# The second layer's gate by GpSimd and ScalarE, and a count that starts at zero with each list of products

## The chip, the cores and the metric

The kernel runs on one core of one Trainium2 chip. The metric is the device time of the program in microseconds (us). The core has five engines with a queue each: TensorE (PE) multiplies matrices, VectorE (DVE) and ScalarE (ACT) work on tiles element by element, GpSimd (POOL) does too, and SyncE (SP) issues the transfers between the memory of the chip and SBUF.

## What is computed

A decoder trunk of two layers on 256 rows of 2048 features, in fp32. Each layer takes three vectors of 2048 numbers from a condition `c`, by one product with a weight of 2048 x 6144:

```
mod = silu(c) @ ada_w[layer] + ada_b[layer]
shift, scale, gate = split(mod, 3)
h = x * (1 + scale) + shift
x = layer_norm(alpha * x + (1 + gate) * mixer(h))
```

The first layer's mixer is a state-space scan (Mamba-2) between two large projections. After it the stream gives one shared set of keys and values (`wk`, `wkv`), and the second layer's mixer is attention over them in three dilations, with a gate path. `gate` of the second layer is needed only in the last step of the kernel.

## The kernel before

Every weight is read in pieces of 128 x 1024 fp32 (512 KB, tile `raw`, six buffers). `split` makes two fp32r tiles of a piece: ScalarE rounds it to `whi` (L126), VectorE subtracts to get the rest `wlo` (L127); each has four buffers. TensorE then multiplies high by high, low by high and high by low. `tm_chunk` (L228 to L230) takes 512 output columns: a piece of it is 12 matmuls of 512 columns. `cm_wide` (L176, L178) takes 256 columns with tiles the other way round.

The products for `mod` are not made on TensorE. A column block of 128 outputs is a tile `araw` (128 x 2048, 1 MB); VectorE multiplies it with `cb_`, which holds silu(c) on every partition, and adds up along the row, in one instruction (`ada_dot`, L310; a second short one reads the accumulator). `ada_load` (L289) fetches the tile; its pools give `araw` two buffers.

`queue(pool, cols)` puts a list of such products into `jobs`, and loads the first at once; each job loads the next column and multiplies its own. `background(n, every)` is called once for each weight piece: it adds `n` to the count `state[0]`, and while that is `every` or more and there are jobs, it takes `every` off and runs one job. There are three lists:

- In the scan's stage, from g = 1 on: the first 8 blocks of the first layer's gate, then a blank and `gate_out(0, 0, 8)`. Rate (1, 8). `drain` at g = 6 runs what is left.
- In the output projection `wout` (chunks n = 0 to 3 of 512 columns, 16 pieces each, the last four of n = 3 held apart without a call), after chunk 0: the other 8 gate blocks, two blanks and `gate_out(0, 8)`, then the first 8 blocks of the second layer's scale and shift. Rate (1, 2).
- In the keys and values: the other 24 blocks of scale and shift, the 16 blocks of the second layer's gate (the second gate), a blank and `gate_out(1)`. Rate (8, 15), over 12 blocks of 4 pieces (`cm_join`) and 4 chunks of 8 (`values[2:]`), 80 calls in all.

`gate_out` adds the bias (L328), transposes the gate on TensorE into a row (L334), copies it (L337) and stores it to the chip's memory (L338); it is read back, spread over the partitions, as `gt` (L86), by which the residual (L851) multiplies a chunk's result. The transpose is pinned behind the weight matmul that was written last before it (`recent[0]`).

The order in which the program is written is not the order in which it runs. `arrange` puts all instructions of the program into an order of its own: a planner with a price for each instruction builds due times from the end, schedules forward, and then tries some 250 seeded random changes of the priorities and keeps what its model likes best. What the written order fixes is the rotation of the buffers and the pins. The planner's price of an operation on GpSimd is

```
return 0.2 + n / 400, 0.2 + n / 370, None, 0
```

in us, for n elements of a row; for ScalarE it is 0.19 + n / 1175 and for VectorE 0.152 + n / 960. When the tiles of the keys and values stage are given back, the pool of the attention stage (`pc2`) takes their place and waits for all their users. `cb_` is overwritten with the attention's bias (L1020) when its last reader is done. At the end of the keys and values stage VectorE and ScalarE also make the second layer's `h` (L1003, L1004, L253, L254).

Of the kernel before, what the change touches and what calls it, by code (L numbers as in the profile page):

```python
# [14 lines left out]
AF = mybir.ActivationFunctionType  # L15
ALU = mybir.AluOpType
# [55 lines left out]
def trunk(ctx, tc, xT, x, ada0, crow, par, cst, bias, lnrow, ada, wdt, win, wsub, wout, wkv, wk, wbin, wbout, out):  # L72
    nc = tc.nc
    del PINS[:]
    V, S, T = nc.vector, nc.scalar, nc.tensor
# [13 lines left out]
    cb_ = cons.tile([P, D], F32, name="cb_")  # L89
# [22 lines left out]
    def note(what, m):  # L112
        noted.setdefault(what, []).append(m.ins.name)
# [35 lines left out]
    state, recent = [0], [None]  # L149
# [136 lines left out]
    def ada_load(pool, layer, kind, ct):  # L286
        raw = pool.tile([P, D], F32, name="araw", bufs=2)
        for c_ in ada_loads(layer, kind, ct):
            m = nc.sync.dma_start(raw[:, c_], ada[layer, KIND.index(kind), ct][:, c_])  # L289
            note((kind, ct, layer), m)  # L290
        return raw

    def ada_parts(layer, kind, ct):

        if layer or kind == "gate" or ct > 1:
            return [slice(0, D)]
        return [slice(768 * i, 768 * i + 768) for i in range(2)] if ct else [slice(0, 512), slice(512, 1024), slice(1024, 1280)]

    def ada_loads(layer, kind, ct):

        return [slice(0, 1024)] if layer == ct == 0 and kind != "gate" else ada_parts(layer, kind, ct)

    def ada_dot(layer, kind, ct, raw, first=None, rest=None):

        j = KIND.index(kind)
        to = mod[layer][:, ct, j:j + 1]
        cuts = ada_parts(layer, kind, ct)
        n = len(cuts)
        if n == 1:
            V.scalar_tensor_tensor(raw, raw, 1.0, cb_, op0=ALU.mult, op1=ALU.mult, accum_out=to)  # L310
            return
        sums = ada_sums(ct, n)
        for i, c_ in enumerate(cuts):
            part = rest[:, j] if ct == 0 and i == 2 else raw[:, c_]
            note(("dot", ct), V.scalar_tensor_tensor(part, part, 1.0, cb_[:, c_], op0=ALU.mult,
                                                     op1=ALU.mult, accum_out=sums[:, j, i:i + 1]))
        if kind == "shift":
            V.tensor_copy(sums[:, :, n], adab[:, 0, ct, 0:2])
            m = mod[0][:, ct, 0:2]
            note(("dot", ct), V.tensor_reduce(m, sums, axis=AX.X, op=ALU.add))  # L320
            note(("dot", ct), V.tensor_tensor(m, first[1 - ct][0][:, :, 0], m, op=ALU.add))

    def ada_sums(ct, n):
        return mod[ct][:, :2 * n + 2, 2].rearrange("p (j i) -> p j i", j=2)
# [14 lines left out]

    def queue(pool, cols):  # L340

        loaded = [ada_load(pool, *cols[0])]

        def step(i):
            raw = loaded.pop(0)
            if i + 1 < len(cols):
                loaded.append(ada_load(pool, *cols[i + 1]))
            ada_dot(*cols[i], raw)

        jobs.extend(lambda i=i: step(i) for i in range(len(cols)))  # L350
# [12 lines left out]
    with ExitStack() as cA:  # L363
# [33 lines left out]
        with ExitStack() as cS:  # L397
# [99 lines left out]
            with ExitStack() as c0:  # L497
# [3 lines left out]
                cols = [(0, kind, kt) for kt in range(KT) for kind in ("scale", "shift")]  # L501
# [12 lines left out]
                def h_step():  # L514

                    _, kind, kt = cols[h_step.i]
                    raw = raws[h_step.i]
                    h_step.i += 1
                    if kind == "scale" and kt % 2 == 0 and kt:
                        fetch_x(kt)  # L520
                    ada_dot(0, kind, kt, raw, first, rest)
                    fetch()
                    while late:
                        late.pop()()
                    if kind == "shift":
                        if kt > 1:
                            ada_bias(0, slice(kt, kt + 1), slice(0, 2))
                        t = pe.tile([P, L], F32, name="htmp")
                        if kt > 1:
                            S.activation(t, xts[kt // 2][:, kt % 2, :], AF.Identity, bias=shift(0, kt), scale=scale(0, kt))  # L530
                            S.activation(hhi[:, kt, :], t, AF.Copy)
                        else:
                            note("hhi", S.activation(hhi[:, kt, :], xts[0][:, kt, :], AF.Identity, bias=shift(0, kt), scale=scale(0, kt)))
                            note(("dot", kt), V.tensor_scalar(t, xts[0][:, kt, :], scale(0, kt), shift(0, kt), op0=ALU.mult, op1=ALU.add))
                        late.append(lambda: note("hlo", V.tensor_tensor(hlo[:, kt, :], t, hhi[:, kt, :].bitcast(F32),
                                                                        op=ALU.subtract)))
# [272 lines left out]
            for g in range(G - 1):  # L809
                if g == 1:  # L810
                    queue(wp1, [(0, "gate", kt) for kt in range(KT // 2)])
                    jobs.extend([lambda: None] + [lambda: gate_out(0, 0, KT // 2)])
                if g == 6:
                    drain()
                if g % 2 == 1:
                    product("bc", g + 1)
                product(*(("xs", g + 1) if g < G - 2 else ("z", G - 2)))
                if rs is not None:
                    stage3(g - 1, rs)
                st1 = stage1(g)  # L820
                if g < G - 2:
                    product(*(("z", g + 1) if g < G - 3 else ("xs", G - 1)))
                rs = stage2(g, *st1)
# [63 lines left out]
        for n in range(4):  # L887
            ps = tm_chunk(wout[n], lambda kt: yhi[kt // 16][:, kt % 16, :], lambda kt: ylo[kt // 4][:, kt % 4, :],
                          nk=2 * KT, rate=(1, 2) if n else (0, 1), pre=None if n else y_ahead,
                          keep=[[pa.tile([P, 1024], F32R, name=f"y{2 * i + j}") for j in range(2)] for i in range(HELD)] if n == 3 else ())  # L890
            if n == 0:
                queue(pn, [(0, "gate", kt) for kt in range(KT // 2, KT)])
                jobs.extend([lambda: None] * 2 + [lambda: gate_out(0, KT // 2)])
                queue(pn, cols1[:8])
            gt = pn.tile([P, 512], F32, name="gt")
            bcast(gt, gated[0], 512 * n)
            c = slice(512 * n, 512 * n + 512)
            for b in range(2):
                xr = pn.tile([P, 512], F32, name="xr", bufs=2)
                nc.sync.dma_start(xr, x[b * P:b * P + P, c])  # L900
                residual(c, ps[b], b, (gt, u[b][:, c]), xr, [st[b][:, n, :]])
            if n == 2:
                root_ahead(2, 1)
# [917 lines left out]
```

## Time and profile before

| | |
|---|---|
| median of 3 runs | 1234.2 us (1233.13 to 1235.16) |
| the profiled execution, its own time | 1232.24 us |
| its span, first to last instruction | 1230.5 us |
| busy PE / DVE / ACT / POOL | 1217.1 / 1056.3 / 698.5 / 0.2 us |
| granted TensorE clock | 1.0 |
| moved by DMA | 358.30 MB, mean 291 GB/s |
| products of `ada_dot` in one instruction (L310) | 92, 2285 ns each |

The span is what the profile shows between the first and the last instruction; some 2 us of the device time lie around it. Line numbers are those of the kernel before. "Idle before" a group is the time that its engine stood before those instructions, with the one that ended the wait behind an arrow.

### The profile page before, as it was taken

To read this page: it belongs to the slowest core of one execution; us is meant where nothing else is said; L and a number is where in the kernel's file an instruction comes from. 1 tells how busy PE (TensorE), PEld (TensorE's weight loads), DVE (VectorE), ACT (ScalarE), POOL (GpSimd) and SP (SyncE) were. 2 spreads that over 40 slices of the span, in tenths; PEclk is the share of its full clock that TensorE was granted. 3 is DMA by queue.
4 is the path that set the end of the run, shared out by engine and by line. 5 is a ranking of instruction groups with operands and counts; after the bars stand their busy time and mean duration, and the time that the engine had idled before them with its cause. 6 is when DMAs were issued, how large, how long until landed. Compare 5 with 4: busy or idle time off the path is not lost.

```text
span 1230.5 us, 17555 instructions
## 1 busy us (share of the span) xinstructions
PE 1217.1 (99%) x6449; PEld 1040.5 (85%) x6449; DVE 1056.3 (86%) x1454; ACT 698.5 (57%) x1041; POOL 0.2 (0%) x4
## 2 busy tenths in 40 slices
PE   8999999999999999999999999999999999999998
PEld 8889888888888888887888788888888889989876
DVE  6998997999999999999857699989986747858677
ACT  4655475687758587963335464435346645545551
POOL 0000000000000000000000000000000000000000
PEclk9999999999999999999999999999999999999999
DMA  9999986978799787789967699999996563462571
GB/s 369 422 420 423 421 326 218 334 252 299 277 354 354 250 277 277 240 330 379 378 209 264 219 378 402 367 385 372 386 376 230 188 190 120 151 193 85 191 272 68
DMA packets 90377, 358.30 MB, mean 291 GB/s; under 512 B 9674, under 2 KB 10410, under 8 KB 77236
## 3 DMA queue, kind: packets, MB, share of 16 engines
q1 hardware_dynamic: 90292, 357.20, 78.9%
q8 instruction: 50, 0.82, 0.3%
q14 instruction: 35, 0.29, 0.1%
HBM read 351.30 MB, written 5.86 MB: 290 GB/s over the span
## 4 chain that ended last, share of the span: by engine, by line
PE 76%; DMA 12%; DVE 8%; ACT 2%; issue 1%; SPq 0%; DVEq 0%; ACTq 0%
PE acc L176 18%; PE acc L229 14%; PE acc L230 14%; PE acc L228 14%; PE acc L178 9%; DMA raw<-in_win 7%; DVE wlo L127 3%; DMA araw<-in_ada 2%; PE py L794 2%; DVE araw L310 2%; DMA xt<-in_xT 2%; DMA raw<-in_wout 1%; DVE ylo L395 1%; PE aux L1056 1%; PE po L1084 1%
## 5 line engine op out<-in xcount | busy, mean ns | idle before, releaser
L126 ACT ACTIVATE whi<-raw 128x1024 fp32r<-128x1024 f32 (+1 forms) x393 | 410.0, 1049 | 348.3 <-PE acc L230 152.9
L127 DVE TENSOR_TENSOR wlo<-raw,whi 128x1024 fp32r<-128x1024 f32 (+1 forms) x393 | 473.1, 1211 | 109.2 <-ACT whi L126 102.8
L229 PE MATMUL acc<-wlo,act 128*128 128x512 f32 x860 | 328.4, 394 | 1.6 <-DVE wlo L127 1.6
L228 PE MATMUL acc<-whi,act 128*128 128x512 f32 x860 | 319.9, 394 | 0.1
L176 PE MATMUL acc<-act,whi 128*128 128x512 f32 x1024 | 267.2, 395 | 0.0
L230 PE MATMUL acc<-whi,act 128*128 128x512 f32 x620 | 233.8, 392 | 0.0
L310 DVE SCALAR_TENSOR_TENSOR araw<-araw,cb__72 128x2048 f32<-128x2048 f32 x92 | 210.2, 2285 | 5.1 <-DMA araw<-in_ada 4.8
L176 PEld LDWEIGHTS acc<-act,whi 128*128 128x128 f32 x1024 | 184.7, 189 | 31.6
L229 PEld LDWEIGHTS acc<-wlo,act 128*128 128x128 f32 x860 | 161.0, 188 | 36.0 <-DVE wlo L127 3.7
L228 PEld LDWEIGHTS acc<-whi,act 128*128 128x128 f32 x860 | 161.1, 188 | 33.1 <-issue 0.5
L178 PE MATMUL acc<-act,wlo 128*128 128x256 f32 x1024 | 150.9, 284 | 0.0
L178 PEld LDWEIGHTS acc<-act,wlo 128*128 128x128 f32 x1024 | 142.0, 190 | 8.6
L230 PEld LDWEIGHTS acc<-whi,act 128*128 128x128 f32 x620 | 116.5, 188 | 24.1 <-issue 0.4
L230 PE MATMUL acc<-whi,ylo 128*128 128x512 f32 x208 | 78.5, 391 | 0.0
L165 PE MATMUL acc<-act,wlo 128*128 128x256 f32 x192 | 49.0, 285 | 0.0
L164 PE MATMUL acc<-act,whi 128*128 128x256 f32 x192 | 47.4, 286 | 1.3 <-ACT whi L126 0.8
L230 PEld LDWEIGHTS acc<-whi,ylo 128*128 128x128 f32 x208 | 39.1, 188 | 7.9
L751 ACT ACTIVATE seg<-seg,cumT 128x128 f32<-128x128 f32 x128 | 39.8, 389 | 1.7 <-DMA seg<-cumd 1.7
L162 PE MATMUL acc<-act,whi 128*128 128x256 f32 x192 | 37.7, 285 | 0.0
L164 PEld LDWEIGHTS acc<-act,whi 128*128 128x128 f32 x192 | 35.1, 191 | 3.1 <-ACT whi L126 1.4
L165 PEld LDWEIGHTS acc<-act,wlo 128*128 128x128 f32 x192 | 35.8, 191 | 1.0 <-DVE wlo L127 0.2
L794 PEld LDWEIGHTS py<-xd,seg 128*128 128x128 f32 x256 | 31.8, 192 | 3.3 <-issue 0.7
(309 smaller groups left out, 1252.4 us busy)
## 6 DMA issues: line engine op xcount, KB each, us to landing
araw<-in_ada SPq DMA_DIRECT2D x92, 1024.0 KB, 7.5
raw<-in_win SPq DMA_DIRECT2D x140, 512.0 KB, 7.4
raw<-in_wout SPq DMA_DIRECT2D x64, 512.0 KB, 4.9
raw<-in_wbin SPq DMA_DIRECT2D x64, 512.0 KB, 3.6
raw<-in_wkv SPq DMA_DIRECT2D x48, 512.0 KB, 5.7
raw<-in_wk SPq DMA_DIRECT2D x48, 512.0 KB, 6.7
moved<-back SPq DMA_DIRECT2D x21, 512.0 KB, 6.4
crow<-in_crow SPq DMA_DIRECT2D x7, 1280.0 KB, 9.4
```

The lines of the kernel that those rows point to most:

```text
L126: a = S.activation(hi[:, c_], raw[:, c_], AF.Copy)
L127: m = V.tensor_tensor(lo[:, c_], raw[:, c_], hi[:, c_].bitcast(F32), op=ALU.subtract)
L164: note("product", T.matmul(o, hi[:, k, c_], ahi[:, kt, :], start=kt == k0 and n % 2 == 0, stop=False, skip_group_check=True))
L165: T.matmul(o, lo[:, k, c_], ahi[:, kt, :], start=False, stop=False, skip_group_check=True)
L176: recent[0] = T.matmul(ps[n], hi[:, k, c_], both[:, kt], start=first, stop=False, skip_group_check=True)
L178: T.matmul(ps[n][:, 0, :], lo[:, k, c_], high[:, kt, :], start=first, stop=False, skip_group_check=True)
L228: begin = T.matmul(ps[b], h_, hi[:, k, :], start=kt == k0, stop=False)
L229: T.matmul(ps[b], h_, lo[:, k, :], start=False, stop=False)
L230: end = T.matmul(ps[b], l_, hi[:, k, :], start=False, stop=kt == k1 - 1)
L310: V.scalar_tensor_tensor(raw, raw, 1.0, cb_, op0=ALU.mult, op1=ALU.mult, accum_out=to)
L751: m = S.activation(seg[:, hh, b, :], seg[:, hh, b, :], AF.Relu, bias=cumT[:, b, h0 + hh:h0 + hh + 1], scale=-1.0)
L794: T.matmul(py[:, e_], segs[hh // 4][:, hh % 4, b, :], xd[:, b, e_], start=True, stop=True)
```

## The change

In `ada_dot`, a gate block of the second layer is multiplied by GpSimd, in place, and then summed by a copy on ScalarE that adds up along the row. The 16 instructions of L310 with their accumulator reads become 16 multiplies on GpSimd and 16 copies with accumulator reads on ScalarE. In `queue`, the count is set to zero with each list, so that what was counted while there were no jobs is forgotten. (The second stage's two lists are queued one right behind the other; both set it.)

```diff
         cuts = ada_parts(layer, kind, ct)
         n = len(cuts)
+        if layer and kind == "gate":
+            nc.gpsimd.tensor_tensor(raw, raw, cb_, op=ALU.mult)
+            S.activation(raw, raw, AF.Copy, accum_out=to)
+            return
         if n == 1:
             V.scalar_tensor_tensor(raw, raw, 1.0, cb_, op0=ALU.mult, op1=ALU.mult, accum_out=to)
             return
...
     def queue(pool, cols):
 
-        loaded = [ada_load(pool, *cols[0])]
+        loaded, state[0] = [ada_load(pool, *cols[0])], 0
```

## The prediction, made before the changed kernel ran

> **What bounds the kernel now.** I read the page's table of engines first, then the busy time by stretches, then the chain of waits where a stretch shows lost TensorE time, and last the groups inside the stretch in which the moved work runs.
>
> ```profile
> PE 1217.1 (99%) x6449; PEld 1040.5 (85%) x6449; DVE 1056.3 (86%) x1454; ACT 698.5 (57%) x1041; POOL 0.2 (0%) x4
> ```
>
> TensorE is busy 99% of the span, but ends of matmuls are modelled, so the count per stretch is the better sign. In the stretches the columns are PE, its weight load, DVE, ACT, POOL (instructions behind x), granted clock, DMA share, GB/s.
>
> ```profile
> 160.00:350.00 190.00, 189.91 (x953) 159.91 (x953) 179.58 (x266) 133.64 (x213) 0.00 (x0) 1.00 0.81 288
> 350.00:550.00 200.00, 199.53 (x1001) 167.09 (x1000) 197.25 (x305) 147.06 (x244) 0.00 (x0) 1.00 0.81 290
> 550.00:600.00 50.00, 48.08 (x212) 39.24 (x211) 44.90 (x49) 19.97 (x21) 0.00 (x0) 1.00 0.96 371
> 600.00:650.00 50.00, 50.00 (x222) 41.43 (x222) 33.28 (x32) 19.68 (x19) 0.00 (x0) 1.00 0.74 266
> 838.00:880.00 42.00, 42.00 (x237) 36.83 (x236) 39.05 (x41) 19.66 (x26) 0.00 (x0) 1.00 1.00 376
> 880.00:921.00 41.00, 41.00 (x182) 33.98 (x182) 35.23 (x32) 18.00 (x19) 0.00 (x0) 1.00 0.99 391
> 921.00:942.00 21.00, 21.00 (x95) 17.40 (x94) 10.59 (x12) 9.12 (x10) 0.00 (x0) 1.00 0.72 239
> 942.00:966.00 24.00, 24.00 (x116) 20.10 (x115) 21.70 (x40) 21.81 (x42) 0.00 (x0) 1.00 0.59 195
> ```
>
> From 600 to 650 us, 222 matmuls, nearly all 512 columns wide, fill 50 us: 0.225 us each is the full pace. From 880 to 921 us there are 182, again 0.225 us each. So where the second gate's products run, TensorE loses nothing, although VectorE is 86 to 93% busy there. The one stretch behind the opening that loses time is 550 to 600 us: 212 matmuls, and 1.92 us idle. Two waits make it up, and the chain of waits runs through them:
>
> ```profile
> 560.98 0.73 PE L229 MATMUL acc<-wlo,act 128*128 128x512 f32 x2 [0.70 <-DVE wlo L127]
> 570.65 0.27 PE L334 MATMUL aux<-cc,mod 128*8 128x128 f32 x1 [1.21 <-DVE mod L328]
> ```
> ```profile
> 563.23 5.96 DMA raw<-in_wout
> ...
> 570.34 0.18 DVE mod L328
> ...
> 570.65 0.27 PE aux L334
> ```
> ```profile
> 566.99 2.29 DVE L310 SCALAR_TENSOR_TENSOR araw<-araw,cb__72 128x2048 f32<-128x2048 f32 x1 [1.58 <-DMA araw<-in_ada]
> ```
>
> L334 is the transpose in `gate_out` for the second half of the first layer's gate. It stands in TensorE's in-order queue before its input is there: the last dot product starts at 566.99, late by its own load, and TensorE stands 1.21 us.
>
> **The reset of the count.** `background` adds to the count also when `jobs` is empty. Counting the calls in the code: 17 before the first list, 104 when the first stage is over, of which its 10 jobs use 80; 24 are left. The second list has a job per 2, so its first call pops (24+1)/2 = 12 jobs: all eight gate products, two blanks, `gate_out` and one more. That pins the transpose only behind the first piece of chunk n=1, and the planner puts it as early as 570.65. From zero, `gate_out`, the 11th job, comes at call 22, the 6th piece of chunk n=2.
>
> ```profile
> 576.46 0.29 SPq L338 DMA_DIRECT2D gated<-row  x1
> ...
> 609.54 0.33 SPq L86 DMA_DIRECT2D gt<-gated  x1
> ```
> ```profile
> 649.63 0.68 DVE L851 TENSOR_TENSOR u<-acc,gt 128x512 f32<-128x512 f32 x1
> ```
> ```profile
> DMA to landing us min/median/max: 5.9/6.3/6.6
> ```
>
> Chunk n=2 ends near 649.6, its first residual. A piece is 12 matmuls, 2.7 us; with ten pieces left after the 6th the transpose cannot stand before about 649.6 - 27 = 623. Behind it come a copy, the store of the row and the load of gt, for which two landings of up to 6.6 us are a generous price: 623 + 14 = 637, 12 us before the residual. On SP's queue the gt load moves from 609.54 to about 630, behind the row's store; weight loads behind it are held for at most one landing, 6.6 us, against six buffers of raw (16 us of TensorE). I cost that at nothing. Gain: the 1.21 us wait goes. What is late next is the 0.70 us wait on wlo, which hangs on a weight load among the same gate loads; it may go as well (bounds of the term: 0 to -1.92; I take -1.2, the wait that the pin removes).
>
> The first list starts at zero instead of 17: its two first products no longer come at once, and its 9th and 10th job fall to `drain` at g=6. The dots are 8 x 2.3 us of VectorE either way, in stretches where TensorE loses 0.09 and 0.47 us; bounds -0.5 to +0.5, taken as 0. The third list starts at zero instead of 24 + 44 - 38 = 30, at 8 per call and 15 per job: its last job, `gate_out(1)`, moves from call 75 of 80 to call 79, that is from the third to the seventh piece of the last chunk, four pieces or 11 us.
>
> ```profile
> L334 PE MATMUL aux<-cc,mod x3: 270/271/272, 427.3 to 949.6; 128*8 128x128 f32 x2, 128*16 128x128 f32 x1
> ```
>
> 949.6 becomes about 960. Its result is read only at the very end, so that costs nothing as long as the sums are there by then.
>
> **The moved products.** Sixteen products leave VectorE. From 840 to 925 us, and from 942 to 966:
>
> ```profile
> L127 DVE TENSOR_TENSOR wlo<-raw,whi 128x1024 fp32r<-128x1024 f32 x31 | 37.9, 1223 | 8.8 <-ACT whi L126 8.1 <-PE acc L178 0.5
> L310 DVE SCALAR_TENSOR_TENSOR araw<-araw,cb__72 128x2048 f32<-128x2048 f32 x16 | 36.6, 2285 | 0.4 <-DMA araw<-in_ada 0.4
> L126 ACT ACTIVATE whi<-raw 128x1024 fp32r<-128x1024 f32 x31 | 32.9, 1062 | 38.3 <-PE acc L230 24.1 <-PE acc L176 11.4 <-DVE wlo L127 1.9
> ...
> L958 ACT ACTIVATE vt<-acc 128x512 f32<-128x512 f32 x4 | 2.4, 592 | 2.2 <-PE acc L230 2.2
> ```
> ```profile
> L254 DVE TENSOR_TENSOR act<-htmp,act 128x256 fp32r<-128x256 f32 x16 | 6.3, 420 | 0.0
> ...
> L1004 DVE SCALAR_TENSOR_TENSOR htmp<-act,mod,htmp 128x256 f32<-128x256 f32 x13 | 5.8, 478 | 0.0
> ```
> ```profile
> 840.50 2.28 DVE L310 SCALAR_TENSOR_TENSOR araw<-araw,cb__72 128x2048 f32<-128x2048 f32 x1
> ```
> ```profile
> 559.71 3.49 DVE L127 TENSOR_TENSOR wlo<-raw,whi 128x1024 fp32r<-128x1024 f32 x3
> ```
> ```profile
> 962.16 0.57 ACT L958 ACTIVATE vt<-acc 128x512 f32<-128x512 f32 x1
> ```
> ```profile
> 919.37 2.28 DVE L310 SCALAR_TENSOR_TENSOR araw<-araw,cb__72 128x2048 f32<-128x2048 f32 x1
> ```
> ```profile
> L797 ACT ACTIVATION_READ_ACCUMULATOR py<-y x16: 185/187/192, 244.9 to 516.1; 128x1 f32 x16
> ```
> ```profile
> L708 DVE RECIPROCAL araw<-araw x1: 944/944/944, 181.7 to 181.7; 128x128 f32<-128x128 f32 x1
> ```
> ```profile
> L1809 POOL MEMSET const-float32-1.0<- 128x1 f32 x1 | 0.1, 98 | 0.0
> ```
>
> VectorE is relieved of 36.6 us. Worth 0: of ACT's 38.3 us of waiting before whi, 35.5 are for TensorE to free buffers, so the split runs ahead of the matmuls and TensorE is at its pace.
>
> ScalarE gains 16 sums. From 512 to 1024 columns an ACT pass grows by 1.062 - 0.592 = 0.47 us, so 2048 take about 2.0 us, plus 0.19 us to read the accumulator: 16 x 2.19 = 35 us. Until 942 it has the room (9 to 20 us busy in 21 to 42). A sum ahead of a whi delays it by 2.2 us at most, less than three buffered pieces (8 us). Only 942 to 966 is full (21.8 of 24); two or three sums that end up there would cost at most what does not fit, 3 x 2.2 - 2.2 = 4.4 us. Bounds 0 to 4.4; I take 0, since the gates may also end behind 966.
>
> GpSimd: no row shows its multiply, only four memsets of one column. Below stands the same product on VectorE, 2.29 us; above, by the dearest VectorE row per element, the reciprocal (0.944 us for 128 columns), 16 x 0.944 = 15 us. I take twice the VectorE row, 4.6 us, as for two operands read one after the other; it is nearest to that row since the arithmetic is the same. Then one product holds a buffer for 4.6 + 2.2 us and its load; 16 x 4.6 = 74 us fit into the 122 us from 840.5 to 963, the end of the last values chunk (its eviction on ACT begins at 962.16); they do not above 7.7 us each. The planner itself reckons 5.3 us (0.2 + 2048/400), so its order leaves room for mine. The Trainium skill (GPSIMD Engine Reference, section 3.1) states 4497 ns for a two-input fp32 op of 2048 columns; with it the sum would be the same.
>
> Who waits: araw has two buffers, and loads wait for the release, now ScalarE's sum. SP's queue stands for VectorE's products 49 times already, up to 5.1 us:
>
> ```profile
> SPq L289 <- DVE araw L310: 102.5, 49, 5.1
> ```
> ```profile
> 921.69 0.33 SPq L1020 DMA_DIRECT2D cb__72<-in_bias  x1
> ```
>
> The load of the bias into `cb_` goes out at 921.69, when the last product has ended; it will wait for GpSimd's last multiply, 20 to 40 us later; its reader comes with the attention, behind the first queries. Taken as 0.
>
> Sum: 1232.2 us (the profiled execution; span 1230.5) - 1.2 = 1231.0. The median of the runs, 1234.2, stands 2.0 above the profiled one, so 1233.0 against 1234.2. A measurement of this kernel tells some 0.2% (2.5 us) from no change, so this counts as no change.
>
> **Rivals.** *Slower: GpSimd's reads and VectorE's two-input operations exclude each other.* Between 840 and 963 VectorE must do 44 low halves (12 pieces of the kv blocks, 32 of values) at 1.14 us from start to start (three in a row take 3.49), and 14 us of L1004 and L254: 64 us, all with two operands in SBUF. With 16 multiplies of m, the serial sum 16m + 64 has 123 us and some 8 us of buffered pieces: it decides from m = 4.2 us. At m = 4.6 it lacks 138 - 131 = 7 us: 1240; at 5.3 us, 18 us: 1251. For it: nothing measured, GpSimd is idle throughout. Against it: the load of araw leaves gaps between multiplies, and the gates could start earlier or end behind 963. The Trainium skill (SBUF — State Buffer, section Who interferes with whom) states this rule: a VectorE instruction with two SBUF inputs and a GpSimd one that reads SBUF share a port, and the second waits for the whole first. By its rule with its 4.5 us the lack is 136 - 131 = 5 us, 1238. The same time follows where GpSimd is merely slow and a sum blocks whi behind it in ScalarE's queue.
>
> *Faster.* Both waits of 550 to 600 go, and the 0.56 us lost from 160 to 550: 1.92 + 0.56 = 2.5 us, 1231.7 or a little below; the planner's noise over a changed list of instructions may add a us in the opening. Against it: there is no more lost time to win until the end.
>
> *The reset does nothing.* The order comes from the planner, not from the jobs; another early wait takes the place of L334's, or gt gets late: 1234.2.
>
> **How the numbers follow.** Forecast 0.40, reset without effect 0.12, slower 0.30, faster 0.18. Each is blurred by about 1.5 us, since the planner's seeded search falls out differently with other instructions. Faster by over 0.2%: 0.20; within: 0.50; slower: 0.30. The range goes from 1230 (faster, with blur) to 1243, which leaves out the far end of the exclusion.
>
> **What would show it.** Right: L334's second transpose behind 620 without a wait, 550 to 600 at 48.08 us of PE or more; POOL with 16 multiplies of 4 to 5.5 us; wlo still 1.22 us. Wrong: L127 of several us beside POOL's multiplies, TensorE idle between 840 and 990, or L334 waiting for ScalarE's last sum near 960.

## The result and the profile after

The changed kernel takes 1248.5 us (median of 5 runs, 1244.63 to 1250.21) against 1233.5 us before (5 runs, 1232.78 to 1235.16): ratio 1.0118, 95% interval 1.01 to 1.0136. It is slower by 15 us; 1233.0 was forecast, and the range ended at 1243. The profiled execution is the quickest of the five: 1244.63 us, span 1242.9, 12.4 us longer than that of before.

From the page after, the engines and four groups (busy us, mean ns, idle before). Behind L310 the changed kernel's line numbers are 4 higher: the transpose L334 is now L338, VectorE's dot product L310 is L314; L310 is GpSimd's multiply, L311 ScalarE's sum.

```profile
PE 1218.3 (98%) x6449; PEld 1038.4 (84%) x6449; DVE 1079.3 (87%) x1422; ACT 725.9 (58%) x1073; POOL 79.6 (6%) x20
...
L127 DVE TENSOR_TENSOR wlo<-raw,whi 128x1024 fp32r<-128x1024 f32 (+1 forms) x393 | 524.0, 1345 | 98.5 <-ACT whi L126 91.7
...
L229 PE MATMUL acc<-wlo,act 128*128 128x512 f32 x860 | 329.1, 394 | 11.1 <-DVE wlo L127 11.0
...
L310 POOL TENSOR_TENSOR araw<-araw,cb__72 128x2048 f32<-128x2048 f32 x16 | 79.4, 4966 | 883.5 <-DVE wlo L127 836.3
...
L311 ACT ACTIVATE araw<-araw 128x2048 f32<-128x2048 f32 x16 | 30.6, 1914 | 37.6 <-POOL araw L310 37.6
```

VectorE was to be relieved of 36.6 us, yet it is busy 23 us longer than before, with 32 instructions fewer. Its low halves L127 have grown. The stretches show where (TensorE alone: busy, matmuls behind x, granted clock, DMA share, GB/s); first before, then after:

```profile
0.00:100.00 100.00, 95.42 (x562) 1.00 1.00 405
...
550.00:600.00 50.00, 48.08 (x212) 1.00 0.96 371
...
836.00:972.00 136.00, 136.00 (x668) 1.00 0.87 318
```
```profile
0.00:100.00 100.00, 94.83 (x565) 1.00 1.00 405
...
550.00:600.00 50.00, 50.00 (x222) 1.00 0.95 369
...
836.00:972.00 136.00, 123.16 (x581) 1.00 0.78 286
```

The 1.92 us of 550 to 600 are won, as forecast, and 12.84 us are lost from 836 to 972, where TensorE had lost none. Net 10.9 of the 12.4 us; 0.6 more is lost in the opening, and the rest is spread. The wait behind it, in the waits of 836 to 972 after (us, times, longest), is TensorE waiting for the low half (the last two rows overlap, the weight load and its matmul):

```profile
POOL araw L310 <- DMA araw<-in_ada: 40.8, 12, 11.7
ACT araw L311 <- POOL araw L310: 37.6, 13, 5.0
...
PEld acc L229 <- DVE wlo L127: 14.9, 11, 2.8
PE acc L229 <- DVE wlo L127: 10.6, 8, 2.3
```

And the timeline of the first multiplies after, GpSimd's rows and then VectorE's:

```profile
836.79 4.88 POOL L310 TENSOR_TENSOR araw<-araw,cb__72 128x2048 f32<-128x2048 f32 x1 [836.35 <-DVE wlo L127]
842.40 4.84 POOL L310 TENSOR_TENSOR araw<-araw,cb__72 128x2048 f32<-128x2048 f32 x1 [0.73 <-DMA araw<-in_ada]
```
```profile
837.11 5.65 DVE L127 TENSOR_TENSOR wlo<-raw,whi 128x1024 fp32r<-128x1024 f32 x1
842.68 5.25 DVE L1008 SCALAR_TENSOR_TENSOR htmp<-act,mod,htmp 128x256 f32<-128x256 f32 x2
847.85 0.41 DVE L199 TENSOR_TENSOR kk<-acc,kk 128x256 f32<-128x256 f32 x1
```

A low half that starts 0.3 us into a multiply ends 1.1 us after it: it has waited for the whole of it and then done its own 1.2 us. The wait counts as busy time of VectorE, which is why that grew. L1008 (L1004 before; two operands in SBUF, 0.48 us in the row of before) does the same at the second multiply: two of them take 5.25 us.

### The profile page after: what moved, and what is told of

Read it like the earlier page. It is cut to its first block, busy times and chain, and to the rows that moved or that the text cites. A ratio compares the mean times of both kernels' runs of the same rounds, so it can differ in the third digit from the quotient of the medians.

```text
span 1242.9 us, 17565 instructions
## 1 busy us (share of the span) xinstructions
PE 1218.3 (98%) x6449; PEld 1038.4 (84%) x6449; DVE 1079.3 (87%) x1422; ACT 725.9 (58%) x1073; POOL 79.6 (6%) x20
## 5 line engine op out<-in xcount | busy, mean ns | idle before, releaser
L127 DVE TENSOR_TENSOR wlo<-raw,whi 128x1024 fp32r<-128x1024 f32 (+1 forms) x393 | 524.0, 1345 | 98.5 <-ACT whi L126 91.7
L314 DVE SCALAR_TENSOR_TENSOR araw<-araw,cb__72 128x2048 f32<-128x2048 f32 x76 | 173.9, 2289 | 2.7 <-DMA araw<-in_ada 2.7
L178 PEld LDWEIGHTS acc<-act,wlo 128*128 128x128 f32 x1024 | 143.3, 190 | 12.0 <-DVE wlo L127 2.4
L310 POOL TENSOR_TENSOR araw<-araw,cb__72 128x2048 f32<-128x2048 f32 x16 | 79.4, 4966 | 883.5 <-DVE wlo L127 836.3
L311 ACT ACTIVATE araw<-araw 128x2048 f32<-128x2048 f32 x16 | 30.6, 1914 | 37.6 <-POOL araw L310 37.6
```

Source lines behind the costliest of these rows:

```text
L127: m = V.tensor_tensor(lo[:, c_], raw[:, c_], hi[:, c_].bitcast(F32), op=ALU.subtract)
L178: T.matmul(ps[n][:, 0, :], lo[:, k, c_], high[:, kt, :], start=first, stop=False, skip_group_check=True)
L310: nc.gpsimd.tensor_tensor(raw, raw, cb_, op=ALU.mult)
```

## The experiments

Theory A: a VectorE instruction with two operands in SBUF and a GpSimd instruction that reads SBUF run one after the other, never together. Rivals: B, ScalarE's sums hold up the high halves behind them in its queue; C, the reset or the order that fell out does it; D, GpSimd shares a rate with VectorE (memory traffic, its writes) and slows it in proportion.

**The two parts apart.** `reset_only` and `move_only` each take one hunk of the diff:

```diff
-        loaded = [ada_load(pool, *cols[0])]
+        loaded, state[0] = [ada_load(pool, *cols[0])], 0
```

> The count is reset, the second gate stays on VectorE. If VectorE and GpSimd shut each other out (exclusion): nothing is lost between 838 and 966 us, L127 stays at 1.21 us on average, the second transpose of gate_out stands behind 615 us without a wait, 550 to 600 us holds 50.0 us of PE; 1231.5 to 1232.8 us. If the loss is one of order, brought by the other lists (order): 1240 us or more here too.

> The second gate goes to GpSimd and ScalarE, the count is not reset. Exclusion: the same stretch loses 11 to 16 us, L127 takes 2 to 3 us on average beside the multiplies, and TensorE's 1.2 us wait for the transpose near 570 us is back; 1246 to 1252 us. Order: about 1233 us.

`reset_only`: 1228.47 us, ratio 0.9966 [0.9954, 0.9978]. `move_only`: 1255.09, ratio 1.0169 [1.0151, 1.0187]. Both times miss the range of the exclusion, by 3 us each, downward and upward; the traces go its way. In `reset_only` TensorE is busy for all 50.00 us of 550 to 600 and all 136.00 of 836 to 972; in `move_only` it loses 2.9 us in the first stretch, and in two parts of the second

```profile
836.00:880.00 44.00, 42.94 (x242) 1.00 0.76 291
880.00:972.00 92.00, 78.84 (x326) 0.96 0.81 287
```

It loses 14.2 us in the two parts together; the last 2.8 of them are a wait of the third transpose for the gate's sums. So the loss belongs to the moved products and not to the reset: the first half of C falls.

**The reset against the planner's seed.** The kernel before and the one with the reset, each with other seeds of the planner's search:

```diff
-    key, best, near = [float(v.i) for v in P[0]], None, random.Random(0)
+    key, best, near = [float(v.i) for v in P[0]], None, random.Random(1)
```

> The kernel before with another seed of the planner's search (1 in place of 0), nothing else: what a mere reshuffle of the order is worth. Exclusion expects 1231 to 1236 us, at most 2.5 us from the kernel before; order expects jumps of 5 us and more to be possible.

> The kernel before with the reset alone, and with the planner's list of tries started from another seed, the one of the run seed1 (1229.4 us without the reset, where a wait of 1.5 us for the gate's remainder stood at 550 to 600 us). If the reset itself is worth its wait: 1227.4 to 1228.5, and 50.00 us of TensorE at 550 to 600. If the 5 us between the kernel before and reset_only were mostly the planner's luck: 1228 to 1233, no better than seed1 by more than 1.5 us.

> The kernel before with a third seed of the planner, nothing else. It sizes what reshuffling alone does: 1228 to 1235, with a loss of 1.5 to 2 us at 550 to 600 us as in the other two kernels without the reset.

> The reset alone with the third seed. If the reset is worth its wait: 1.2 to 2 us less than seed2 and no loss at 550 to 600 us. If the planner's luck decides: anywhere within 4 us of seed2, on either side.

| seed | without reset | with reset | difference | lost at 550 to 600, without / with |
|---|---|---|---|---|
| 0 | 1233.7 | 1228.5 | -5.2 | 1.92 / 0.00 |
| 1 | 1229.4 | 1230.4 | +1.0 | 2.15 / 0.00 |
| 2 | 1232.7 | 1229.9 | -2.8 | 1.80 / 0.00 |

The loss at 550 to 600 goes with every seed, and the mean difference, -2.3 us, is about its size; but the seed alone moves the kernel by up to 4.3 us (`seed1`, where at most 2.5 was expected), so a single pair says little. Three pairs that lie between -5.2 and +1.0 do not prove a gain in the whole time; they prove that the wait goes.

**ScalarE's sums without GpSimd.** `dve_mult`: VectorE multiplies in place, ScalarE sums, reset kept; also with the other seed.

```diff
-            nc.gpsimd.tensor_tensor(raw, raw, cb_, op=ALU.mult)
+            V.tensor_tensor(raw, raw, cb_, op=ALU.mult)
```

> As the changed kernel, but VectorE makes the 16 multiplies (without a sum), ScalarE still sums. Exclusion: GpSimd is idle, so no low half takes over 1.3 us; 1231 to 1235 us. If ScalarE's 16 sums of 2.1 us, standing ahead of the rounding in its queue, are what TensorE waits for (sums): 1240 to 1249 us, with waits of whi behind L311.

> VectorE multiplies, ScalarE sums, reset, with the planner's tries started from the other seed (1236.12 with the first one; the reset alone 1228.47 and 1230.38 with the two seeds). If the sums as such cost: 1234 to 1238 and TensorE's loss between 836 and 972 of about 3 us again. If the 7.6 us were the order that fell out: 1229 to 1233.

1236.12 us, ratio 1.0021 [1.0011, 1.0031], between the two ranges that were expected, and with seed 1 1231.68, ratio 0.9992 [0.9981, 1.0003], in the range of the order. The low halves are as short as before (mean 1.22 us). What the sums cost against the reset alone is +7.6 us with one seed and +1.3 with the other; what the trace of 836 to 972 shows of it is 3.1 and 0.9 us. Of the 7.6, another 2.6 us stand in the first 100 us, where no sum runs (TensorE busy 93.83 us in `dve_mult`, 96.42 in `reset_only`). The 3.1 are one wait behind two sums that stand ahead of three high halves (ScalarE's timeline in `dve_mult`):

```profile
890.29 1.92 ACT L311 ACTIVATE araw<-araw 128x2048 f32<-128x2048 f32 x1 [0.66 <-DVE araw L310]
892.11 0.19 ACT L311 ACTIVATION_READ_ACCUMULATOR araw<-araw 128x1 f32 x1
892.20 2.94 ACT L126 ACTIVATE whi<-raw 128x1024 fp32r<-128x1024 f32 x3
```

B exists, then, at 1 to 3 us in place, within what was bounded (0 to 4.4). It is not the 15: between `dve_mult` and the changed kernel only the engine that multiplies differs, and with it the order that the planner finds. That is worth 12.4 us (1248.51 - 1236.12), with the other seed 20.7 (below), of which some 4 stand in the first 100 us (`after_seed1` has 1.1 us less of busy TensorE there and a granted clock of 0.97).

**GpSimd without the sums, and the other order.** `short_sum` sums 128 columns of each product only; `after_seed1` is the changed kernel with seed 1.

```diff
-            S.activation(raw, raw, AF.Copy, accum_out=to)
+            S.activation(raw[:, :P], raw[:, :P], AF.Copy, accum_out=to)
```

> The changed kernel with ScalarE's sum over 128 of the 2048 columns (leaves out most of each sum of the second gate), so that its 16 sums of 1.9 us become short while GpSimd's multiplies stay. If exclusion alone loses the 12.8 us of TensorE between 836 and 972: still 11 to 14 us lost there, 1243 to 1249 in all, VectorE's low halves of 5 us as before. If the sums are part of the loss (about 3 us by the kernel with VectorE's multiplies, more if a sum that waits holds the high halves): 5 to 10 us lost, 1237 to 1243.

> The changed kernel with the other seed. If the loss is the exclusion, it doesn't hang on one order: 1243 to 1252, 10 to 16 us of TensorE lost between 836 and 972, low halves of 5 us beside the multiplies. If it was one bad order: under 1240.

`short_sum`: 1247.17 us, ratio 1.0121 [1.0097, 1.0145]; `after_seed1`: 1252.35, ratio 1.0158 [1.0142, 1.0173], where 13.6 us are lost from 836 to 972. With short sums, from 836 to 972:

```profile
836.00:972.00 136.00, 127.93 (x588) 0.96 0.80 294
```

TensorE stands 8.1 us, in the middle of what the second view expected; yet the time is in the first view's range, 1.3 us under the changed kernel, since the granted clock is 0.96 here. Added over the six slices of 4 us that show under 1.00, each weighted with TensorE's busy time in it, that is 4.0 us of work lost at the lower clock: 12.1 us again. So the loss needs neither long sums nor one order: C is out.

One form of B stays in `short_sum`. A sum, short or long, waits in ScalarE's queue for GpSimd's multiply (37.1 us here, 37.6 in the changed kernel) and holds the high halves behind it. In the changed kernel a sum waits 5.01 us for a multiply that ends at 926.56, the high half behind it starts at 928.51, and the low half made from that falls into the next multiply:

```profile
927.11 5.01 POOL L310 TENSOR_TENSOR araw<-araw,cb__72 128x2048 f32<-128x2048 f32 x1 [0.54 <-DMA araw<-in_ada]
```
```profile
929.59 4.75 DVE L127 TENSOR_TENSOR wlo<-raw,whi 128x1024 fp32r<-128x1024 f32 x2 [1.94 <-ACT whi L126]
```

TensorE stands 1.64 us for it, until 933.26. How much of the 12.8 us such a sum adds to the exclusion, no run separates; the next run shows no cost of such waits by themselves.

**What in VectorE's instruction.** `psum_low` lets the low halves of the four values chunks read a row of zeros in PSUM in place of the high half in SBUF, in two halves of 512 (the subtraction of the high half is left out there). The low halves of the key and value blocks before them, up to 880, stay as they were.

```diff
+            if other[0] is not None:
+                for h_ in parts(1024, 2):
+                    V.tensor_tensor(lo[:, h_], raw[:, h_], other[0], op=ALU.subtract)
+                continue
```

> As the changed kernel, but in the last four chunks of values a low half is two subtractions of 512 columns whose second operand is a tile of zeros in PSUM (the low halves are thereby not the rest of the rounding). GpSimd multiplies as before. If the second SBUF operand is what excludes: these subtractions take 0.69 us each beside a multiply as anywhere, and only the kv blocks before (838 to 878) and the short operations at the end can still wait; 1229 to 1237 us. If any VectorE operation stands while GpSimd reads: 1245 us or more.

1234.81 us, ratio 1.0012 [1.0003, 1.0021], as the first view expected: 13.7 us less than the changed kernel, with the same 16 multiplies. Groups of 836 to 972 (L129 has the PSUM operand, L131 two in SBUF, L316 is GpSimd's multiply), then TensorE's stretches:

```profile
L316 POOL TENSOR_TENSOR araw<-araw,cb__72 128x2048 f32<-128x2048 f32 x16 | 74.8, 4680 | 871.9 <-DMA raw<-in_wk 833.8 <-DMA araw<-in_ada 36.1 <-ACT araw L317 2.0
L129 DVE TENSOR_TENSOR wlo<-raw,aux 128x512 fp32r<-128x512 f32 x64 | 41.1, 683 | 32.1 <-PE acc L235 32.1
L131 DVE TENSOR_TENSOR wlo<-raw,whi 128x1024 fp32r<-128x1024 f32 x16 | 35.3, 2220 | 5.0 <-ACT whi L126 5.0
```
```profile
836.00:880.00 44.00, 40.04 (x219) 0.96 0.74 270
880.00:972.00 92.00, 92.00 (x415) 1.00 0.86 318
```

One kernel, both halves of A: to 880, where the second operand is in SBUF, low halves of 2.2 us and a loss; behind it, with an operand in PSUM, none, and none of the 64 subtractions takes more than 0.69 us. The edit also frees these low halves from waiting for the high half, which could make them earlier but not shorter; and TensorE needs the high halves as before. In ScalarE's queue sums still wait for multiplies, 15.4 us from 880 to 972, and TensorE loses nothing there.

**What in GpSimd's instruction.** `pool_one` replaces the product by a multiplication with a constant (the second operand is left out), `pool_write` by two memsets (nothing is read; the products are zero). One run each.

> As the changed kernel, but GpSimd multiplies by a constant and so reads one operand, not two (the gate's sums are thereby those of the weights alone). If any GpSimd read excludes: L127 is stretched up to that instruction's length plus 1.1 us. If only a two-operand GpSimd instruction does: L127 stays at 1.22 us in all of the stretch.

> As the changed kernel, but in place of each multiply GpSimd sets the tile to zero twice: it writes and reads nothing (the gate's sums are zero). If reads exclude: L127 stays at 1.22 us throughout, TensorE loses no more than some 3 us between 838 and 966, as with the sums alone; 1228 to 1237 us. If writes exclude too: L127 up to the length of a memset plus 1.1 us.

```profile
L310 POOL TENSOR_SCALAR araw<-araw 128x2048 f32<-128x2048 f32 x16 | 90.7, 5668 | 870.2 <-DVE mod L332 838.4 <-DMA araw<-in_ada 28.7 <-ACT whi L126 3.0
L127 DVE TENSOR_TENSOR wlo<-raw,whi 128x1024 fp32r<-128x1024 f32 x45 | 88.1, 1987 | 27.5 <-ACT whi L126 27.5
```
```profile
L127 DVE TENSOR_TENSOR wlo<-raw,whi 128x1024 fp32r<-128x1024 f32 x49 | 59.9, 1225 | 51.7 <-ACT whi L126 50.8 <-PE acc L178 0.9
L311 POOL MEMSET araw<- 128x2048 f32 x26 | 47.2, 1814 | 924.9 <-ACT whi L126 839.6 <-DMA araw<-in_ada 65.9 <-ACT act L253 9.4
```

One operand read is enough (1241.14 us, low halves of 1.99 us on average); writes alone leave the low halves at 1.225, so D falls in the form of writes. The time of `pool_write`, 1256.68, refutes what was expected of it, for a reason of its own: the gates end later (the last memset starts at 1001.2 us; the last multiply of the changed kernel at 958.6), and TensorE stood at the row that they end in, with a granted clock of 0.82 from 972 to 1010. That the planner put them later because it reckons 2 x 5.3 us for two memsets that take 1.8 each is likely, and not shown.

```profile
PE aux L339 <- DVE mod L333: 14.7, 1, 14.7
```

**Smaller pieces.** `quarters` splits the product into four of 512 columns, so that a low half waits for a short instruction only.

```diff
-            nc.gpsimd.tensor_tensor(raw, raw, cb_, op=ALU.mult)
+            for c_ in parts(D, 4):
+                nc.gpsimd.tensor_tensor(raw[:, c_], raw[:, c_], cb_[:, c_], op=ALU.mult)
```

> As the changed kernel, but each multiply on GpSimd is four of 512 columns (some 1.2 us each in place of 4.9). If a low half that meets a multiply waits for the end of that one instruction (exclusion by instruction), it now takes at most some 2.6 us in place of 5.7; TensorE's three buffered pieces cover that, and the stretch 838 to 966 loses under 5 us: 1229 to 1238 us. If what counts is the sum of the work at a shared port (sharing), or if GpSimd keeps the port from part to part, the loss stays: 1245 us or more.

1246.65 us, ratio 1.01 [1.008, 1.0121]: nothing won, where the exclusion by instruction was expected to give 1229 to 1238. The group of 836 to 972 and two waits of 880 to 972 say why:

```profile
L311 POOL TENSOR_TENSOR araw<-araw,cb__72 128x512 f32<-128x512 f32 x64 | 114.7, 1827 | 850.4 <-DMA raw<-in_wk 835.2 <-DMA araw<-in_ada 13.1 <-ACT araw L312 2.1
```
```profile
ACT araw L312 <- POOL araw L311: 33.2, 10, 4.2
DVE wlo L127 <- ACT whi L126: 30.7, 12, 4.2
```

The waits became short, but now both engines take turns: a quarter that takes 1.27 us at its shortest takes 1.83 on average, GpSimd needs 7.2 us for a product, and the sum, which stands in ScalarE's queue ahead of the next high halves, waits for it. Turn-taking moved the wait to another engine. From 836 to 972, the low halves are longer than alone by 52 us in the changed kernel and 33 here, GpSimd's instructions by 7 and 34: 59 against 67 us together.

**The engines by themselves.** `bench` leaves out the whole computation: stretches between barriers on buffers of 128x2048.

> Not the transformer: stretches set apart by barriers, on 128x2048 buffers, to price the two engines by themselves. VectorE subtract 128x1024 with both operands in SBUF: alone; beside GpSimd's 128x2048 multiply; beside GpSimd's one-operand multiply by a constant; beside GpSimd's memset. Beside GpSimd's multiply also: VectorE subtract 128x512 with one operand in PSUM, VectorE one-operand multiply by a constant, VectorE reduction, ScalarE copy. GpSimd's multiply alone. Exclusion theory (an instruction of VectorE with two SBUF operands and one of GpSimd that reads never run together): the subtract takes 1.0 to 1.2 us alone, and beside the multiply each pair shows one subtract of about 4.5 to 5.7 us per multiply, the rest short, with the multiply stretched by at most one subtract; the same beside the one-operand multiply; beside the memset 1.0 to 1.2 as alone. The subtract with PSUM, the reduction and ScalarE's copy are as long beside the multiply as alone. Rival, a shared rate (both slow down in proportion): all subtracts beside the multiply show the same lengthened time, 1.5 to 2.5 us, and the multiply is well over 4.6. Open: whether VectorE's one-operand multiply by a constant is delayed as well; between 0.5 us (no) and 4.6 us (yes).

Groups of its page. VectorE's subtract with two SBUF operands (128x1024) stands alone at L95, beside GpSimd's multiply at L103, beside its one-operand multiply at L123, beside memsets at L128; a subtract of 512 with PSUM beside the multiply at L108; a one-operand multiply at L113 beside it and at L136 alone; ScalarE's copy at L118 beside it. (A reduction takes 1.22 us beside it, each of eight the same; no run has it alone.) GpSimd's multiply is alone at L98.

```profile
L103 DVE TENSOR_TENSOR vo<-va,vb 128x1024 f32<-128x1024 f32 x6 | 19.9, 3312 | 9.6 <-SPq L91 9.4
L98 POOL TENSOR_TENSOR go<-ga,gb 128x2048 f32<-128x2048 f32 x2 | 9.0, 4495 | 23.0 <-SPq L91 22.9
L123 DVE TENSOR_TENSOR vo<-va,vb 128x1024 f32<-128x1024 f32 x6 | 17.3, 2881 | 9.6 <-SPq L91 9.4
...
L101 POOL TENSOR_TENSOR go<-ga,gb 128x2048 f32<-128x2048 f32 x3 | 16.2, 5416 | 0.3 <-SPq L91 0.2
L113 DVE TENSOR_SCALAR vo<-va 128x1024 f32<-128x1024 f32 x8 | 13.9, 1737 | 3.8 <-SPq L91 3.6
L95 DVE TENSOR_TENSOR vo<-va,vb 128x1024 f32<-128x1024 f32 x6 | 7.3, 1225 | 10.1 <-SPq L91 9.9
...
L118 ACT ACTIVATE so<-sa 128x1024 f32<-128x1024 f32 x6 | 6.3, 1057 | 59.6 <-SPq L91 59.4
...
L128 DVE TENSOR_TENSOR vo<-va,vb 128x1024 f32<-128x1024 f32 x6 | 7.3, 1225 | 1.0 <-SPq L91 0.8
...
L136 DVE TENSOR_SCALAR vo<-va 128x1024 f32<-128x1024 f32 x8 | 5.6, 694 | 0.3
L108 DVE TENSOR_TENSOR vo<-va,ps 128x512 f32<-128x512 f32 x8 | 5.5, 687 | 0.4
```

The trace's summary of L103 gives the spread:

```profile
L103 DVE TENSOR_TENSOR vo<-va,vb x6: 1224/3312/5399, 32.6 to 51.4; 128x1024 f32<-128x1024 f32 x6
```

Three subtracts of up to 5.4 us for three multiplies, the others 1.22: not slowed in proportion, but held for a whole instruction, and the multiply in its turn for one subtract (5.42 against 4.50). ScalarE's copy is as long as in the kernel before (1.06 us). D falls in every form. Six subtracts and three multiplies take 20.0 us together; end to end they would take 7.5 + 13.5 = 21.0, so "never together" holds but for 1 us. VectorE's multiplication by a constant, whose question was open, is held as well (1.74 against 0.69 on average, the longest 4.87), though it reads one operand: A as stated is too narrow on VectorE's side.

## Why the prediction was wrong

**The bound and the reset were read rightly.** The second transpose now stands at 618.37 us without a wait (5 us ahead of the 623 worked out as the earliest, half of it because chunk n=2 ends at 647.05), the third at 973.11 (about 960 forecast; 957.0 in `reset_only`); 550 to 600 is full. The term of -1.2, bounds 0 to -1.92, measured -1.92 there. The sums were taken as 0 with bounds 0 to 4.4; the traces show 3.1 and 0.9 us without GpSimd.

**The step that failed** is "VectorE is relieved of 36.6 us", together with GpSimd costed by its own time alone (4.6 us, and 74 us of multiplies into 122). In its place the runs showed VectorE busy 23.0 us longer: from 836 to 972 a low half takes 2.43 us on average in place of 1.22, and TensorE loses 12.84 us there. The duration was right: 4.50 us alone, 4.59 to 5.63 in place. Whether the two engines can work at once was never priced in the sum, only as a rival at 0.30, though both of its halves stood there as rows: 44 low halves with two operands in SBUF, and a stretch with 86 to 93% of VectorE busy. No row of before showed GpSimd reading, so nothing spoke against the rival either; its "gaps" do exist (GpSimd waits 40.8 us for its loads) and did not save it. The Trainium skill (SBUF — State Buffer, Who interferes with whom) states the rule without reservation, and here the traces agree: 5.65 us for a low half beside a multiply, 0.69 for the subtractions with an operand in PSUM beside one (`psum_low`, `bench`), 1.225 beside memsets.

**The rival was mis-sized too.** It lacked 136 to 138 us against 131, 5 to 7 us, so 1238 to 1240. Lost was more: 8.1 us of empty TensorE in `short_sum`, where the sums are short, 12.8 with the whole sums. The sum in series assumes that 8 us of buffered pieces even out everything; TensorE stood nine times between 836 and 972, 0.3 to 2.3 us each, always for a low half; that the buffers had run low where a multiply met it is an argument, not a measurement. (At the measured mean of 4.97 us the formula gives 79.5 + 64 - 131 = 12.5, near the 12.8, but that is no confirmation: the 4.97 contains time in which GpSimd waited for VectorE, which the 64 counts already.) Two things came on top that no term held: the granted clock behind stalls (4.0 us in `short_sum`), and the planner's luck, reckoned at 1.5 us and measured at up to 4.3. The changed kernel's median lies 3.9 us above its profiled execution; two of its other runs have a mean clock of 0.996 against 0.999, worth 3.7 us, but one has 0.999 and is as long, so this spread is only partly explained.

## To carry to other kernels

Before work is moved to an idle GpSimd, list what VectorE does in that stretch: where its instructions have two operands in SBUF, GpSimd's reading time is to be added to VectorE's, not set beside it, and the move can make the busy engine busier. Splitting the work into small pieces shortened each wait and not their sum here, while an operand in PSUM took the wait away. And where an order is found by a seeded search, price a change of one or two us with several seeds; here a pin that truly removed a 2 us wait showed as -5.2, +1.0 and -2.8. No version was faster than the reset alone (1228.5 to 1230.4 over three seeds), but one seed without it, at 1229.4, is as fast.

## What was not expected of the hardware

A stall of TensorE can cost more than its length. In `move_only`, after 4.33 us without a matmul, those of 512 columns follow at 0.43 us from start to start in place of 0.23, until about 908:

```profile
904.82 0.80 PE L229 MATMUL acc<-wlo,act 128*128 128x512 f32 x1 [4.33 <-DVE wlo L127]
905.41 0.63 PE L230 MATMUL acc<-whi,act 128*128 128x512 f32 x1
905.84 0.63 PE L228 MATMUL acc<-whi,act 128*128 128x512 f32 x1
...
908.33 0.40 PE L230 MATMUL acc<-whi,act 128*128 128x512 f32 x1
908.57 0.40 PE L228 MATMUL acc<-whi,act 128*128 128x512 f32 x1
```
```profile
904.00:908.00 4.00, 3.18 (x8) 0.60 0.61 188
908.00:912.00 4.00, 4.00 (x18) 0.97 0.97 332
```

A stall of 2.41 us in `psum_low` was followed by the same (granted clock 0.69 from 868 to 872), and one of 2.07 us in `short_sum` (0.70 from 848 to 852); one of 2.33 us in the changed kernel, at 900, was not. The Trainium skill (TensorE: Matmul & The Clock Gate, The HAM clock gate) has half the clock after an idle window of some 3.4 us, and windows that run by themselves, so that it matters where in one a stall falls. The halving agrees, and its length is some 3.4 us (0.40 of the first four us above and 0.03 of the next, at half speed); that a shorter stall can be enough is what these runs add.

GpSimd's multiplication of one operand by a constant takes longer than its product of two: 5.37 us at its shortest in `pool_one` against 4.50 (`bench`, alone), both for 2048 columns.
